# Depthwise convolution tiles moved from tap-by-tap VectorE operations to products on TensorE's column quarters

## The chip, the cores and the metric

One core of a Trainium2 chip runs the whole program. The metric is the device time of one execution in microseconds (us), lower is better. The engines named here are TensorE (PE, with its weight loads as PEld), VectorE (DVE), ScalarE (ACT), GpSimd (POOL) and SyncE (SP), whose queue issues most DMAs.

## The reference

Two blocks follow each other. The first has two layers over 528 tokens (16 of them meta tokens, padded further in the reference); each layer makes one projection, splits it, runs a causal depthwise convolution of width 31 over 512 channels and a sparse attention (top-k keys per query), and joins both through `w_out`. The second block has window attention, a gated linear attention and 16 experts. The change touches the convolution of the first block:

```
proj = jnp.einsum('bld,de->ble', h, w_in[l])
a, g, zc, q, k, v, za, qi, ki, wi = jnp.split(proj, IN_SPLITS, axis=-1)
u = a * jax.nn.sigmoid(g)
u = lax.conv_general_dilated(u, w_dw[:, None, :], window_strides=(1,),
        padding=[(CONV_WIDTH - 1, 0)], dimension_numbers=('NWC', 'WIO', 'NWC'),
        feature_group_count=D_CONV) + b_dw
u = jax.nn.silu(layer_norm(u, ln_g, ln_b))
return u * jax.nn.silu(z)
```

So each of the 512 channels is convolved by itself: 31 multiply-adds per output, no sum over channels.

## The kernel before

Channels lie on partitions, tokens along the free axis. The 512 convolution channels are four tiles of 128 (c = 0 to 3). The first layer carries 528 tokens through this part, the second 512. `p_ag(c)` computes one tile: the projections a and g (96 products at L181 with split weights: a weight tile `raw` is loaded at L151, ACT casts it to `wh` at L159, DVE takes the rest `wl` at L160), then ACT's `th` (L339) and DVE's `u` (L340), the gated input, with zeros ahead of it. Then `conv_tap(c, j)` is called 31 times and builds `cv[:, c]` in one of two ways:

- tiles in the set `pconv`: ACT multiplies (L323) and POOL adds (L325), tile after tile. `pconv` is (0, 1, 2) in layer 0 and (0, 1) in layer 1.
- the other tiles: one DVE operation per tap (L328 for the first, L330 for the other 30). These are tile 3 in layer 0, and tiles 3 and 2 in layer 1.

Everything else of the layer competes for the same engines. `topk` (L413, L414) is a long series on DVE. The attention runs in four pieces; in each, scores go through `burst` (L252, L258) into `pidx`, DVE reduces them (L585, `smb`), ACT takes the exponential (L590), PE transposes (L558) and multiplies by v (L565), and DVE ends the piece at L507 (`yas`). The tail of a layer reads `cv` (L650, L655), then the product with `w_out` follows. The weight tiles move in a fixed order on SP's queue, each load waiting until the buffer `raw` is free, which is when `wl` of an earlier tile is done.

The order on each engine is not that of the source: pieces of the program have levels (`plan`, `levels`, `go`), and a scheduler lays the instructions out by level before the run. In layer 0 the convolution tiles come in the order 2, 3, 1 after tile 0, with topk between them; in layer 1 in the order 1, 0, 3, 2. PE's two buffers named `pp` hold projection results until they are read.

Of the kernel before, what the change touches and what calls it, by code (L numbers as in the profile page):

```python
# [13 lines left out]
AF = mybir.ActivationFunctionType  # L14
ALU = mybir.AluOpType
AX = mybir.AxisListType
# [6 lines left out]
L = S + NM  # L23
KT = D // 128
W31 = 31
PAD = W31 - 1
ALPHA = 4.0 ** 0.25
TOPK = min(256, L // 4)
BIG = 1e30
# [39 lines left out]
class Net:  # L69
# [202 lines left out]
    def layer(self, l):  # L272
        nc, I = self.nc, self.I
        w_in, w_out = I["w_in"][l], I["w_out"][l]
        hT = self.hT
        q0 = 0 if l == 0 else NM
        T = L - q0
# [18 lines left out]
            nc.tensor.transpose(pcv[:, c, :], cw[:, c * 128:(c + 1) * 128], self.ident[:34, :34])  # L296
        cvec = self.sb([128, 4, 34], "cvec")
        nc.vector.tensor_copy(cvec, pcv)
        taps = self.sb([128, 4, 31], "taps")
        nc.vector.tensor_scalar(taps, cvec[:, :, 0:31], 0.5, None, op0=ALU.mult)  # L300

        pgb = self.sb([16, 128], "pgb", "rl", 3)
        nc.scalar.dma_start(pgb[0:8], I["post_ln_g"][l:l + 1].rearrange("o (t p) -> (o t) p", p=128))
# [11 lines left out]
        prod = []  # L315

        def conv_tap(c, j):
            src = u[:, c, j + q0:j + q0 + T]
            if c in pconv:
                if not prod:  # L320
                    prod.append(self.sb([128, 2, L], "prod", "zM"))
                pr = prod[0][:, j % 2, :T] if j else cv[:, c, :]
                nc.scalar.activation(pr, src, AF.Identity, scale=taps[:, c, j:j + 1], bias=0.0 if j else cvec[:, c, 31:32])  # L323
                if j:
                    nc.gpsimd.tensor_tensor(cv[:, c, :], cv[:, c, :], pr, op=ALU.add)  # L325
                return
            if j == 0:
                nc.vector.tensor_scalar(cv[:, c, :], src, taps[:, c, 0:1], cvec[:, c, 31:32], op0=ALU.mult, op1=ALU.add)  # L328
            else:
                nc.vector.scalar_tensor_tensor(cv[:, c, :], src, taps[:, c, j:j + 1], cv[:, c, :], op0=ALU.mult, op1=ALU.add)  # L330

        def p_ag(c):
            self.go("ag")
            ps = []
            for n in ("a", "g"):
                raw = self.load_w(w_in, WCOL[n] + 128 * c, 128)
                ps.append(self.proj(self.split_w(raw), 128, hT, KT, fsegs))
            th = self.sb([128, L], "th", "rl", 3)
            nc.scalar.activation(fseg(th), ps[1], AF.Tanh, scale=0.5)  # L339
            nc.vector.scalar_tensor_tensor(fseg(u[:, c, PAD:]), fseg(th), 1.0, ps[0], op0=ALU.add, op1=ALU.mult)  # L340
            self.go("conv")
            for j in range(W31):
                conv_tap(c, j)

# [74 lines left out]
        def topk_short(i):  # L419
            w = NM + 128 * (i + 1)  # L420
            out = w - TOPK
            acc = accs[i][:, :w]
            tk = self.sb([128, 3, w + 8], "tk", "up")
            n, e, c = (tk[:, k] for k in range(3))
            m8 = self.sb([128, 8], "m8", bufs=4)
            v = self.sb([128, 1], "tkv")
            pad = -out % 8
            nc.vector.memset(n[:, w:w + 8], 3e38 if pad else NEG_MARK)
            nc.vector.tensor_scalar(n[:, :w], acc, -1.0, None, op0=ALU.mult)
            for r in range((out + pad) // 8):  # L430
                nc.vector.max(m8, n[:, :w + pad])
                if r < (out + pad) // 8 - 1:
                    nc.vector.match_replace(n[:, :w + pad], m8, n[:, :w + pad], NEG_MARK)
            nc.vector.tensor_scalar(m8[:, 7:8], m8[:, 7:8], -1.0, None, op0=ALU.mult)
            n, e, c = (t[:, :w] for t in (n, e, c))
            nc.vector.tensor_scalar(n, acc, m8[:, 7:8], 0.0, op0=ALU.is_gt, op1=ALU.add, accum_out=v)
            nc.vector.tensor_scalar(v, v, -1.0, float(TOPK), op0=ALU.mult, op1=ALU.add)
            nc.vector.tensor_scalar(e, acc, m8[:, 7:8], None, op0=ALU.is_equal)
            nc.vector.tensor_tensor_scan(c, e, e, 0.0, op0=ALU.add, op1=ALU.bypass)
            nc.vector.scalar_tensor_tensor(e, c, v, e, op0=ALU.is_le, op1=ALU.mult)  # L440
            nc.vector.tensor_add(n, n, e)
            nc.vector.scalar_tensor_tensor(acc, n, BIG, self.c1[:, 3, L - w:], op0=ALU.mult, op1=ALU.add)
# [1232 lines left out]
    def first_block(self):  # L1675
        nc, I = self.nc, self.I
        self.ident = self.sb([128, 128], "base")
        nc.sync.dma_start(self.ident, I["c_base"])
        z = self.sb([128, 4, D], "z", "qk")
        zM = self.sb([NM, D], "zM")  # L1680
        nc.sync.dma_start(zM, I["meta_tokens"])
        for i in range(4):
            nc.sync.dma_start(z[:, i, :], I["x"][0, 128 * i:128 * (i + 1), :])
        self.c1 = self.sb([128, 4, L], "c1")
        nc.scalar.dma_start(self.c1, I["c_1"].rearrange("p (a b) -> p a b", a=4))
        self.new_hT()
        self.transposes_to(*self.hT, 0, zM, NM)
        for i in range(4):
            self.transposes_to(*self.hT, NM + 128 * i, z[:, i, :])
        for l in range(2):  # L1690
            self.cur = None
            self.layer(l)
# [26 lines left out]
```

## Time and profile before

| what | value |
|---|---|
| median of 3 runs | 1849.26 us (1848.18 to 1853.11) |
| the profiled execution, its own time | 1850.64 us |
| its span | 1848.8 us |
| mean granted clock of TensorE in it | 0.965 |

The profiled execution's time is its span and 1.8 us around it. Stages named in the text are stretches of the span in us: layer 0's attention ends near 327, layer 1's near 688, and the second block fills the rest.

### The profile page before, as it was taken

To read this page: it belongs to the slowest core of one execution; us is meant where nothing else is said; L and a number is where in the kernel's file an instruction comes from. 1 tells how busy PE (TensorE), PEld (TensorE's weight loads), DVE (VectorE), ACT (ScalarE), POOL (GpSimd) and SP (SyncE) were. 2 spreads that over 40 slices of the span, in tenths; PEclk is the share of its full clock that TensorE was granted. 3 is DMA by queue.
4 is the path that set the end of the run, shared out by engine and by line. 5 is a ranking of instruction groups with operands and counts; after the bars stand their busy time and mean duration, and the time that the engine had idled before them with its cause. 6 is when DMAs were issued, how large, how long until landed. Compare 5 with 4: busy or idle time off the path is not lost.

```text
span 1848.8 us, 27815 instructions
## 1 busy us (share of the span) xinstructions
PE 1686.7 (91%) x11323; PEld 1342.3 (73%) x11323; DVE 1010.8 (55%) x1947; ACT 765.4 (41%) x1310; POOL 238.0 (13%) x161
## 2 busy tenths in 40 slices
PE   6989989889998899799999999999899988888888
PEld 6989877889997789799888899999533332233246
DVE  3899994666998985775533445543401221012044
ACT  3874656447666554634355444322300000000026
POOL 1620863000068400000000000000000000000000
PEclk9999989999999899899989999999999999999999
DMA  6213111121222112222122248556799999999961
GB/s 194 69 47 93 46 46 46 30 70 59 69 61 79 46 47 81 89 69 91 36 63 75 76 143 288 158 211 230 280 421 421 421 420 421 421 420 421 419 273 46
DMA packets 147104, 323.35 MB, mean 175 GB/s; under 512 B 13034, under 2 KB 102826, under 8 KB 128672
## 3 DMA queue, kind: packets, MB, share of 16 engines
q1 hardware_dynamic: 142112, 310.54, 45.3%
q10 hardware_dynamic: 3856, 7.37, 1.1%
q0 software_dynamic: 1008, 3.67, 0.5%
q8 instruction: 89, 1.46, 0.3%
q14 instruction: 39, 0.32, 0.1%
HBM read 305.22 MB, written 16.25 MB: 174 GB/s over the span
## 4 chain that ended last, share of the span: by engine, by line
PE 58%; DMA 17%; DVE 15%; ACT 6%; issue 3%; POOL 1%; SPq 0%; ACTq 0%; DVEq 0%; POOLq 0%
PE pp L181 36%; PE pp L1571 7%; DMA rawe<-in_w_exp_down 7%; DMA rawe<-in_w_exp_gate 4%; DMA rawe<-in_w_exp_up 4%; DVE cv L330 3%; PE pp L1631 2%; DVE wl L160 2%; POOL cv L325 1%; ACT wh L159 1%; DVE smb L585 1%; PE po L565 1%; DVE acc L414 1%; DMA rawe<-in_w_ple_gate 1%; DVE m L413 1%
## 5 line engine op out<-in xcount | busy, mean ns | idle before, releaser
L325 POOL TENSOR_TENSOR cv<-cv,prod 128x528 f32<-128x528 f32 (+1 forms) x150 | 231.1, 1541 | 393.7 <-ACT prod L323 385.0
L1571 PE MATMUL pp<-rawe,xf 128*64 128x512 f32 x1024 | 247.8, 600 | 12.7 <-DMA rawe<-in_w_exp_gate 8.6
L181 PE MATMUL pp<-hTh,wh 128*128 128x264 f32 (+2 forms) x1056 | 227.4, 296 | 22.9 <-ACT th L339 8.0
L159 ACT CAST wh<-raw 128x1024 fp32r<-128x1024 f32 (+2 forms) x149 | 150.9, 1016 | 229.7 <-PE pp L181 204.0
L181 PE MATMUL pp<-hTl,wh 128*128 128x264 f32 (+2 forms) x1056 | 226.9, 295 | 0.1
L181 PE MATMUL pp<-hTh,wl 128*128 128x264 f32 (+2 forms) x1056 | 224.6, 293 | 0.0
L160 DVE TENSOR_TENSOR wl<-raw,wh 128x1024 fp32r<-128x1024 f32 (+2 forms) x149 | 187.5, 1259 | 65.9 <-ACT wh L159 59.2
L181 PEld LDWEIGHTS pp<-hTh,wh 128*128 128x128 f32 (+1 forms) x1056 | 170.9, 195 | 29.7 <-ACT th L339 9.3
L1571 PEld LDWEIGHTS pp<-rawe,xf 128*64 128x64 f32 x1024 | 76.8, 137 | 158.5 <-issue 131.0
L181 PEld LDWEIGHTS pp<-hTl,wh 128*128 128x128 f32 (+1 forms) x1056 | 170.7, 195 | 7.5 <-issue 6.7
L181 PEld LDWEIGHTS pp<-hTh,wl 128*128 128x128 f32 (+1 forms) x1056 | 169.8, 194 | 2.2 <-issue 1.6
L181 PE MATMUL pp<-xTh,wh 128*128 128x264 f32 (+1 forms) x752 | 156.3, 289 | 2.8 <-ACT op L1000 2.3
L181 PE MATMUL pp<-xTl,wh 128*128 128x264 f32 (+1 forms) x752 | 156.5, 288 | 0.5 <-DVE xTl L1095 0.5
L181 PE MATMUL pp<-xTh,wl 128*128 128x264 f32 (+1 forms) x752 | 155.2, 286 | 0.0
L1571 PE MATMUL pp<-rawe,hid 128*64 128x512 f32 x512 | 127.6, 616 | 18.6 <-DMA rawe<-in_w_exp_down 18.1
L1460 DVE SCALAR_TENSOR_TENSOR Y<-pp,per,Y 128x512 fp32r<-128x512 f32 x16 | 12.0, 749 | 232.7 <-ACT Y L1459 232.7
L1428 POOL DMA_INDIRECT xr<-xrows,slots x7 | 6.7, 958 | 993.2 <-DMA xrows<-zr 699.5
L323 ACT ACTIVATE prod<-u,taps 128x528 f32<-128x528 f32 (+1 forms) x150 | 107.6, 729 | 50.4 <-POOL cv L325 50.0
L181 PEld LDWEIGHTS pp<-xTh,wh 128*128 128x128 f32 (+1 forms) x752 | 116.8, 190 | 4.8 <-ACT op L1000 2.5
L181 PEld LDWEIGHTS pp<-xTl,wh 128*128 128x128 f32 (+1 forms) x752 | 116.2, 189 | 3.1 <-issue 2.2
L181 PEld LDWEIGHTS pp<-xTh,wl 128*128 128x128 f32 (+1 forms) x752 | 116.1, 189 | 0.8 <-issue 0.8
L1571 PEld LDWEIGHTS pp<-rawe,hid 128*64 128x64 f32 x512 | 40.6, 141 | 99.5 <-issue 61.0
(504 smaller groups left out, 2972.1 us busy)
## 6 DMA issues: line engine op xcount, KB each, us to landing
rawe<-in_w_exp_gate SPq DMA_DIRECT2D x53, 1024.0 KB, 16.3
rawe<-in_w_exp_up SPq DMA_DIRECT2D x52, 1024.0 KB, 15.0
rawe<-in_w_exp_down SPq DMA_DIRECT2D x51, 1024.0 KB, 19.6
raw<-in_w_in SPq DMA_DIRECT2D x45, 1024.0 KB, 5.3
rawe<-in_w_exp_down SPq DMA_DIRECT2D x26, 512.0 KB, 15.5
rawe<-in_w_exp_up SPq DMA_DIRECT2D x22, 512.0 KB, 16.2
rawe<-in_w_exp_gate SPq DMA_DIRECT2D x22, 512.0 KB, 17.4
raw<-in_w_in SPq DMA_DIRECT2D x20, 512.0 KB, 6.5
```

The costliest lines, as they stand in the source:

```text
L159: nc.scalar.copy(wh, raw_view)
L160: nc.vector.tensor_sub(wl, raw_view, wh.bitcast(F32))
L181: nc.tensor.matmul(ps[:m, s, x:min(x + k, n)], a[:, t, :m], b[:, c0 + x:min(c0 + x + k, c1)], start=(t == 0 and pi == 0 and x == 0), stop= ...
L323: nc.scalar.activation(pr, src, AF.Identity, scale=taps[:, c, j:j + 1], bias=0.0 if j else cvec[:, c, 31:32])
L325: nc.gpsimd.tensor_tensor(cv[:, c, :], cv[:, c, :], pr, op=ALU.add)
L330: nc.vector.scalar_tensor_tensor(cv[:, c, :], src, taps[:, c, j:j + 1], cv[:, c, :], op0=ALU.mult, op1=ALU.add)
L413: nc.vector.max(m8, acc)
L414: nc.vector.match_replace(acc, m8, acc, NEG_MARK)
L565: nc.tensor.matmul(po[:, h, :], pT[:, x * (i + 1) + j, :], v[:, j, h * 64:(h + 1) * 64], start=first[0], stop=False, skip_group_check=True)
L585: nc.vector.tensor_tensor_reduce(sm[:, x, :], pss[p][:, x, :], acc[:, NM:w], 1.0, mi[:, h:h + 1], ALU.add, ALU.max, mx[:, h:h + 1])
L1571: nc.tensor.matmul(ps[a, s, :], x[:, a], r, start=(t == 0 and k == 0), stop=(t == KT - 2 and k == 1), skip_group_check=True)
L1631: nc.tensor.matmul(ps[k][:, k, :], a[:, t, :], wp[t][:, w, k * 512:(k + 1) * 512], start=(t == 0 and pi == 0), stop=(t == KT - 1 and pi == 2))
```

## The change

`pconv` now says only which tiles go tap by tap on ACT and POOL. The other three go to `conv_products(c)`. It writes the convolution as products with diagonal operands. The 31 taps are padded to 32 with one zero (so the zeros ahead of `u` grow by one column), and read as 8 rounds of 4 taps. For each group g of 32 channels the 128 rows of the array hold four copies of these channels, each shifted by one more token (`us`, made by 16 DMAs from SP of 32 partitions each), and the operand for round e is 128 x 32: four diagonals stacked, with the taps 4e to 4e+3 (`cwt`, made by 16 small products and one DVE operation). A product of 32 output channels uses 32 columns of the array, a quarter; the four groups go to the four quarters. A tile takes two halves of the tokens x 8 rounds x 4 groups = 64 float32 products, in two `burst`s of 32, into one `pp` buffer, and ACT copies the sum with the bias to `cv`.

```diff
-PAD = W31 - 1
+PAD = W31
+CQ = 4
...
         def conv_tap(c, j):
-            src = u[:, c, j + q0:j + q0 + T]
-            if c in pconv:
...
-            if j == 0:
-                nc.vector.tensor_scalar(cv[:, c, :], src, taps[:, c, 0:1], cvec[:, c, 31:32], op0=ALU.mult, op1=ALU.add)
-            else:
-                nc.vector.scalar_tensor_tensor(cv[:, c, :], src, taps[:, c, j:j + 1], cv[:, c, :], op0=ALU.mult, op1=ALU.add)
...
+        def conv_products(c):
+            n = T // 2
+            nx = T + W31 + 1 - CQ
+            pt = self.ps([128, 4, 8], "pcv")
+            for g in range(4):
+                for k in range(CQ):
+                    nc.tensor.matmul(pt[32 * k:32 * k + 32, g, :], self.ident[:, 32 * g:32 * g + 32], taps[:, c, k::CQ], start=True, stop=True)
+            w = self.sb([128, 4, 8, 32], "cwt", "k2l")
+            nc.vector.tensor_tensor(w.rearrange("p g e c -> p (g e) c"), self.mask32[:, None, :].to_broadcast([128, 32, 32]),
+                                    pt.rearrange("p g e -> p (g e)")[:, :, None].to_broadcast([128, 32, 32]), op=ALU.mult)
+            us = [self.sb([128, 2, nx], "us", "sm", 2) for _ in range(2)]
+            for g in range(4):
+                for k in range(CQ):
+                    nc.sync.dma_start(us[g // 2][32 * k:32 * k + 32, g % 2, :], u[32 * g:32 * g + 32, c, k + q0:k + q0 + nx])
+            ps = self.ps([128, 2, 512], "pp", "pp", 2)
+            for k in range(2):
+                products = []
+                for e in range(8):
+                    for g in (3, 2, 1, 0):
+                        x0 = CQ * e + n * k
+                        products.append(((ps[32 * g:32 * g + 32, k, :n], w[:, g, e, :], us[g // 2][:, g % 2, x0:x0 + n]),
+                                         dict(start=e == 0, stop=e == 7, skip_group_check=True)))
+                self.burst(products)
+            nc.scalar.activation(cv[:, c, :].rearrange("p (k n) -> p k n", k=2), ps[:, :, :n], AF.Identity, scale=1.0, bias=cvec[:, c, 31:32])
...
             self.go("conv")
+            if c not in pconv:
+                conv_products(c)
+                return
```

The copies `us` take both buffers of the tag `sm`, which the attention's `smb` uses too. The rest of the diff moves two small tiles to other buffers and makes the 32-wide mask once.

The change moves instructions on the engines that meet here. On VectorE, at the end of layer 1's topk, the order of before has the attention's first reductions (L585) among the last steps of topk:

```order
L549 TENSOR_REDUCE mi<-smm_6270 128x8
L414 MATCH_REPLACE acc<-m_6079,acc 128x532
L413 MAX m_6042<-acc 128x8
L585 ISA smb,mx<-pidx,acc,mi 128x384
L585 ISA mx 128x1
L413 MAX m_6079<-acc 128x8
```

In the order of the change, topk ends first (L441 to L443), then come weight remainders, the two `u` of tiles 3 and 2 with `cwt` between them, and only then the attention's first reduction (now L612):

```order
L441 MATCH_REPLACE acc<-m_6227,acc 128x532
L442 TENSOR_SCALAR acc<-acc 128x272
L442 TENSOR_SCALAR acc<-acc 128x528
L443 TENSOR_TENSOR acc<-acc,c_72 128x272
L443 TENSOR_TENSOR acc<-acc,c_72 128x528
L161 TENSOR_TENSOR wl<-raw,wh 128x1024
L364 SCALAR_TENSOR_TENSOR u<-th,pp 128x528
L339 TENSOR_TENSOR cwt<-mask_146,pcv 128x1024
L161 TENSOR_TENSOR wl<-raw,wh 128x1024 x2
L364 SCALAR_TENSOR_TENSOR u<-th,pp 128x528
L612 ISA smb,mx<-pidx,acc,mi 128x384
```

So the attention of layer 1 moves behind both product tiles on VectorE. On PE, behind the projections of tile 3 and eight pairs of products of tile 2, the 64 products of tile 3 (`pp<-us,cwt`) now stand, with projections on both sides (the last rows before them and the first behind them):

```order
L182 MATMUL pp<-hTl,wh 128x264 x2
L182 MATMUL pp<-hTh,wl 128x264 x2
L253 MATMUL pp<-us,cwt 32x256
L259 MATMUL pp<-us,cwt 32x256 x31
L253 MATMUL pp<-us,cwt 32x256
L259 MATMUL pp<-us,cwt 32x256 x31
L182 MATMUL pp<-hTh,wh 128x264 x2
L182 MATMUL pp<-hTl,wh 128x264 x2
```

Those of tile 2 stand 65 instructions of the listing's L182 kind and one pair of scores later, and layer 0 has one such place, 16 products behind the projections of its tile 3. On ACT the copy of the sum (L354) of layer 1's tile 3 stands among the taps of the ACT tiles (L325), and the cast of a later weight tile (L160, the second half of tile 2's projections) behind five more taps:

```order
L325 ACTIVATE prod<-u,taps 128x512 x17
L354 ACTIVATE cv<-pp,cvec 128x512
L325 ACTIVATE prod<-u,taps 128x512 x5
L160 CAST wh<-raw 128x1024
L325 ACTIVATE prod<-u,taps 128x512 x2
L160 CAST wh<-raw 128x1024
L363 ACTIVATE th<-pp 128x528
L354 ACTIVATE cv<-pp,cvec 128x512
```

So an instruction that PE's projections wait for now stands behind one that waits for the convolution's products.

## Rows read from the trace of the kernel before

**Rows 1.** The page, section 1: busy us, share of the span, instructions.

```profile
PE 1686.7 (91%) x11323; PEld 1342.3 (73%) x11323; DVE 1010.8 (55%) x1947; ACT 765.4 (41%) x1310; POOL 238.0 (13%) x161
```

**Rows 2.** Windows: PE, PEld, DVE, ACT, POOL busy (x), PEclk, DMA share, GB/s.

```profile
200.00:225.00 25.00, 22.75 (x172) 21.74 (x172) 25.00 (x57) 17.96 (x34) 23.75 (x15) 0.92 0.14 43
...
250.00:275.00 25.00, 20.34 (x115) 18.16 (x116) 24.89 (x44) 10.44 (x22) 16.53 (x11) 0.80 0.13 43
...
600.00:625.00 25.00, 18.95 (x126) 16.63 (x124) 24.89 (x30) 14.47 (x34) 19.57 (x13) 0.90 0.14 43
```

**Rows 3.** Tile `cv`: line, engine, out<-in xcount: ns min/median/max, first and last start.

```profile
L325 POOL TENSOR_TENSOR cv<-cv,prod x150: 1268/1468/3352, 40.0 to 623.6; 128x528 f32<-128x528 f32 x90, 128x512 f32<-128x512 f32 x60
L330 DVE SCALAR_TENSOR_TENSOR cv<-u,taps,cv x90: 726/752/1883, 204.0 to 672.6; 128x512 f32<-128x512 f32 x60, 128x528 f32<-128x528 f32 x30
```

**Rows 4.** Windows of 25 us, L330 alone: one row, and the sum of eleven.

```profile
200.00:225.00 25.00, 7.87 (x7) 0.92 0.14 43
...
...
sum 275.00, DVE 89.64; mean DVE 8.15
```

**Rows 5.** Windows: two full stretches of projections, and the stretches around the tiles.

```profile
140.00:170.00 30.00, 30.00 (x254) 29.71 (x253) 29.38 (x81) 12.16 (x24) 0.00 (x0) 1.00 0.28 72
196.90:327.30 130.40, 115.94 (x827) 103.80 (x825) 103.30 (x213) 83.53 (x167) 81.26 (x52) 0.92 0.13 41
360.00:390.00 30.00, 30.00 (x251) 29.91 (x250) 17.17 (x40) 8.43 (x15) 0.00 (x0) 1.00 0.34 106
545.50:705.10 159.60, 142.02 (x1064) 128.20 (x1062) 140.38 (x303) 94.87 (x187) 68.07 (x45) 0.95 0.19 60
```

**Rows 6.** Timeline of PE at the second block's router products (start, us, instruction).

```profile
1261.23 1.06 PE L1317 MATMUL plog<-res,wr 128*32 128x512 f32 x6
1262.22 0.39 PE L181 MATMUL pp<-mh,wh 128*128 128x264 f32 x1
```

**Rows 7.** The same place: timeline of the weight loads, and the tile `plog`.

```profile
1261.23 0.15 PEld L1317 LDWEIGHTS plog<-res,wr 128*32 128x32 f32 x6
...
L1317 PEld LDWEIGHTS plog<-res,wr x16: 106/108/110, 1261.2 to 1289.0; 128*32 128x32 f32 x16
L1317 PE MATMUL plog<-res,wr x16: 592/604/617, 1261.2 to 1289.4; 128*32 128x512 f32 x16
```

**Rows 8.** Timeline of SP's queue: small copies between weight loads.

```profile
148.78 1.25 SPq L481 DMA_DIRECT2D vM<-vm  x2
153.02 0.37 SPq L151 DMA_DIRECT2D raw<-in_w_in  x1
```

**Rows 9.** DMA view: issues, KB each, median us from issue to landing.

```profile
vM<-vm SPq DMA_DIRECT2D x16, 4.0 KB, 2.2
h1d<-h SPq DMA_DIRECT2D x8, 256.0 KB, 2.3
```

**Rows 10.** Windows of 5 us around a stop of PE (the column behind POOL is PEclk).

```profile
110.00:115.00 5.00, 2.26 (x11) 2.27 (x11) 5.00 (x8) 3.16 (x5) 2.64 (x2) 0.65 0.01 2
115.00:120.00 5.00, 5.00 (x30) 5.00 (x30) 4.94 (x9) 4.32 (x9) 0.13 (x1) 0.66 0.16 33
```

**Rows 11.** Timeline of VectorE in layer 0: tile 3's `u`, and the end of topk.

```profile
200.72 0.69 DVE L340 SCALAR_TENSOR_TENSOR u<-th,pp 128x528 f32<-128x528 f32 x1
...
235.64 1.23 DVE L416 TENSOR_TENSOR acc<-acc,c 128x528 f32<-128x528 f32 x1
```

**Rows 12.** Timeline of VectorE in layer 1: `wl` behind topk, and the last two `u`.

```profile
575.77 1.22 DVE L160 TENSOR_TENSOR wl<-raw,wh 128x1024 fp32r<-128x1024 f32 x1
587.60 0.73 DVE L340 SCALAR_TENSOR_TENSOR u<-th,pp 128x528 f32<-128x528 f32 x1
615.85 0.69 DVE L340 SCALAR_TENSOR_TENSOR u<-th,pp 128x528 f32<-128x528 f32 x1
```

**Rows 13.** Source L507 in layer 0 and in layer 1: first and last end of an attention piece.

```profile
L507 DVE TENSOR_TENSOR yas<-po,rs x4: 670/678/692, 235.0 to 326.7; 128x512 f32<-128x512 f32 x4
L507 DVE TENSOR_TENSOR yas<-po,rs x4: 674/678/682, 594.1 to 686.8; 128x512 f32<-128x512 f32 x4
```

More of the change, by code (lines that the diff above doesn't have):

```diff
@@ L298, in layer @@
         nc.vector.tensor_copy(cvec, pcv)
-        taps = self.sb([128, 4, 31], "taps")
-        nc.vector.tensor_scalar(taps, cvec[:, :, 0:31], 0.5, None, op0=ALU.mult)
+        taps = self.sb([128, 4, W31 + 1], "taps")
+        nc.vector.memset(taps[:, :, 0:1], 0.0)
+        nc.vector.tensor_scalar(taps[:, :, 1:], cvec[:, :, 0:31], 0.5, None, op0=ALU.mult)
         pgb = self.sb([16, 128], "pgb", "rl", 3)
@@ L317, in conv_tap @@
         def conv_tap(c, j):
-            src = u[:, c, j + q0:j + q0 + T]
-            if c in pconv:
[L320 to L326, printed above, removed]
@@ L327, in conv_tap @@
-            if j == 0:
-                nc.vector.tensor_scalar(cv[:, c, :], src, taps[:, c, 0:1], cvec[:, c, 31:32], op0=ALU.mult, op1=ALU.add)
-            else:
-                nc.vector.scalar_tensor_tensor(cv[:, c, :], src, taps[:, c, j:j + 1], cv[:, c, :], op0=ALU.mult, op1=ALU.add)
+            src = u[:, c, j + 1 + q0:j + 1 + q0 + T]
+            if not prod:
+                prod.append(self.sb([128, 2, L], "prod", "zM"))
+            pr = prod[0][:, j % 2, :T] if j else cv[:, c, :]
+            nc.scalar.activation(pr, src, AF.Identity, scale=taps[:, c, j + 1:j + 2], bias=0.0 if j else cvec[:, c, 31:32])
@@ new lines, in conv_tap @@
+            if j:
+                nc.gpsimd.tensor_tensor(cv[:, c, :], cv[:, c, :], pr, op=ALU.add)
+        def conv_products(c):
[22 more added lines that the diff above has]
+            nc.scalar.activation(cv[:, c, :].rearrange("p (k n) -> p k n", k=2), ps[:, :, :n], AF.Identity, scale=1.0, bias=cvec[:, c, 31:32])
@@ L425, in topk_short @@
             m8 = self.sb([128, 8], "m8", bufs=4)
-            v = self.sb([128, 1], "tkv")
+            v = self.sb([128, 1], "tkv", "am")
             pad = -out % 8
@@ L1689, in first_block @@
             self.transposes_to(*self.hT, NM + 128 * i, z[:, i, :])
+        self.mask32 = self.sb([128, 32], "mask32", "xr")
+        nc.vector.tensor_reduce(self.mask32, self.ident.rearrange("p (s c) -> p c s", s=4), axis=AX.X, op=ALU.add)
         for l in range(2):
```

## The prediction

> **What bounds the kernel now.** I read the page's busy shares first: PE 91% of the span, DVE 55% [rows 1]. These are averages, so I next cut the stretches where the convolution runs into windows. There the picture turns: in 200 to 225, 250 to 275 and 600 to 625 VectorE is busy for 24.9 to 25.0 us of 25, while PE is busy for 19 to 23 us and its granted clock stands at 0.80 to 0.92 [rows 2]. PE waits for VectorE there, and the convolution is one of the reasons: 90 operations of line L330, 726 to 1883 ns each [rows 3], 89.6 us in all by windows [rows 4], about 30 in layer 0 (one tile) and 60 in layer 1 (two), plus the three first taps.
>
> How much could PE gain at most? Where PE is never idle at full clock, it retires 254 or 251 instructions in 30 us, 0.118 to 0.12 us each [rows 5]. Between the end of layer 0's `u` of tile 3 and the end of its attention, 196.9 to 327.3, it retires 827 in 130.4 us [rows 5]: 97.6 us of work at 0.118, so 32.8 us are idle or run at a low clock. From 545.5 to 705.1, where layer 1's product with `w_out` starts, it retires 1064 in 159.6 us [rows 5]: 125.6 us of work, 34.0 us slack. Together 66.8 us: that is what the change can win, before it adds anything.
>
> **The change, part by part.** *Removed:* 93 VectorE operations, 92 us with the first taps. VectorE was full there, so its other work moves up; but what this is worth is limited by the slack above, and only if PE doesn't get new waits.
>
> *Products on PE.* The trace has no float32 product of 264 columns on a quarter, but a near row: the router's products are 128 x 32 by 512 columns, float32, on four quarters. Six records (each product leaves two records, one per pass, and some are missing) begin at 1261.23 and end 1.06 us later, and the next product starts at 1262.22 [rows 6], so four products of 512 columns take 0.99 us side by side, although one record alone is 604 ns [rows 7]. With 264 or 256 columns I scale to 0.51 us a round. A tile has 2 halves x 8 rounds = 16 rounds: 8.2 us. The lower bound is the same (the rows have no faster one); one after another it would be four times that, 33 us, a rival below. The 16 small products for `cwt` are 8 columns each; at the 0.12 us of any PE instruction at most 2 us, I take 1. So 9.2 us for a tile, 27.6 for three.
>
> The Trainium skill, page "TensorE: Matmul & The Clock Gate", section "Part 3: Packing small matmuls — row/col tiling", says that a weight load overlaps products in flight only when the row group differs; here every product uses all 128 rows. By it each quarter's load would stand in the open. The row says otherwise: six loads of 106 to 110 ns lie within 0.15 us while the products run [rows 7], so I add nothing for loads. By the rule the sum would be about 10 us more; that case is a rival below.
>
> *The copies.* This is new on the path: between `u` and the first product there are now 16 DMAs from SP. Two small copies issue in 1.25 us on this queue, a weight load in 0.37 us [rows 8], so 16 take 5.9 to 10.0 us; a copy lands 2.2 us (4 KB) to 2.3 us (256 KB) after its issue [rows 9]. That bounds `u` to first product at 8.1 to 12.2 us; I take 10.5, nearer to the small copies, which they resemble. On SP they are queued behind the weight loads, which wait for `wl`, and the next weight load waits behind all 16. `cwt`, of the size of `wl` (1.22 us [rows 12]), lies beside the copies.
>
> What covers this? In the order, PE has 16 projection products behind tile 3's projections in both layers, then the burst: 2 us of cover. PE is in order, so it stands for 8 to 9 us. After a stop of this kind the granted clock fell to 0.65 and 0.66 for two windows of 5 us [rows 10], the lower of the two levels for a good part of them: 3.4 us lost. A tile thus costs 9 + 3.4 + 9.2 us, about 22.
>
> *Layer 0 (tile 3).* `u` is made at 200.7 now [rows 11]; I put it at 199, as the attention's reductions no longer stand ahead. Copies land at 209.5, the burst ends near 221. On ACT the copy L354 stands behind 19 taps that POOL paces at 1.27 to 1.47 us each [rows 3], 24 to 28 us, so to 223 to 227, and the cast of a weight tile behind it and four exponentials; PE has 32 products, 4 us, before it needs that cast: 1 to 7 more us of waiting, I take 5. Sum 27 against a slack of 32.8, so PE alone would end at 196.9 + 97.6 + 27 = 321.5 instead of 327.3. The attention starts later, but with VectorE free: topk ended at 236.9 [rows 11]; without the taps before it (7.87 us until 225 [rows 4], some 4 behind it) and the reductions it ends near 220. The last three pieces took 235.0 to 326.7, 91.7 us [rows 13], with about 20 us of the tile's taps among them; with a first piece of some 20 us the end lies between 220 + 20 + 72 = 312 and 332. I take 325: **-2 us**, bounds -6 (PE) to +10.
>
> *Layer 1 (tiles 3 and 2).* Here the order matters more. `u` of tile 3 now stands directly behind topk and one `wl`: 577 instead of 587.6 [rows 12], 10 us earlier. Copies land at 587.5, the products end near 598 with the low clock. Then the cast for tile 2's second half stands on ACT behind L354 and five taps: 0.8 + 6, 605. PE finishes tile 2's projections near 611, `u` follows at 613 or 614 (now 615.8 [rows 12], so all 10 us are gone). Copies land at 624, with 2 us of PE work (17 products) as cover; the products end near 634. VectorE idles through most of 578 to 634, as all attention stands behind the second `u`. Before that point PE has done 3 x 96 projections and some 30 others of the stretch, 318 x 0.118 = 37.5 us; 125.6 - 37.5 = 88 us remain to `w_out`. Without any further wait it starts at 722, 17 us later than at 705.1. The lower bound is lower: copies at 8.1 and no low clock give 4 to 5 us back for each tile, so +6. Some waits remain, as four attention pieces must run in these 88 us, which took 552 to 686.8 with taps in between (the last three 92.7 us [rows 13]); 6 us more is a choice between none and the 20 that would make the pieces as long as before less the taps. **+23 us**, bounds +6 to +38.
>
> *Sum.* -2 + 23 = +21 on the profiled execution's 1850.6: 1871.6. The profile lies 1.4 above the median of the runs, so 1870. The bounds give 1849 to 1897.
>
> **The rivals.** *The freed VectorE wins (faster).* If the copies land within about 3 us of `u`, with the 2 us of cover PE hardly stops, the clock stays up, and of the 66.8 us slack only 27.6 is spent: up to 39 us faster, 1810; half of it carried, 1830. It decides at a gap of 3 us from `u` to the first product. For it: VectorE full [rows 2]. Against: the issue times [rows 8]. Chance 0.18.
>
> *The stalls fall into idle time that stood anyway (no change).* If PE's stops replace the waits for VectorE one for one, layer 0 ends 6 earlier and layer 1 6 later, near 1849. For it: the slack of 34 us is spread over the same stretch. Chance 0.11.
>
> *The quarters don't run side by side.* Then a tile costs 33 us, 25 more for each of three: about 1945. The router's row speaks against it; but its products number 8, here 64 stand in a row and accumulate. Chance 0.05.
>
> *Weight loads in the open.* If a load waits for the products in flight, each of 32 passes pays 0.108 us [rows 7]: 3.5 us a tile, 10 in all, 1880. Chance 0.04. It is what the Trainium skill's sentence above amounts to.
>
> **How the numbers follow.** My forecast has 0.62, with a range of its own of 1852 to 1896. For 8 in 10 the range must reach down to the half-carried gain: 1832 to 1896; the serial quarters and the better half of the gain stay out. A measurement of this kernel tells about 0.3%, 5.5 us, from no change. Faster: the first rival and a little of the second, 0.19. Same: most of the second and the edge of the forecast, 0.11. Slower: the rest, 0.70.
>
> **What would show it.** In the changed profile: L344 in SP's queue 16 times in 6 to 10 us and PE idle for 8 to 9 us before L253/L259 `pp<-us,cwt`, released by the DMA; that burst 8 to 12 us; a lower granted clock behind it; VectorE with idle stretches near 580 to 630; the first L612 of layer 1 near 630; layer 0's last L534 near 325. It is wrong if the DMA gap is short, if the burst takes another time than 8 us at full clock, or if the attention behind it runs much faster, or slower, than I let it.

## The result, and the profile after

The changed kernel takes 1897.34 us (median of 4 runs, 1894.89 to 1901.11) against 1850.52 for the kernel before: ratio 1.0254, 95% interval 1.0230 to 1.0278. It is 47 us slower where 20 were forecast, just above the range. One execution of e4 below took 2732 us at a mean granted clock of 0.567; the ratios leave it out.

The page's first section answers to [rows 1]. VectorE gave up 83.5 us, PE took 17 more, and the span grew by 48.1:

```profile
PE 1703.8 (90%) x11803; PEld 1354.8 (71%) x11803; DVE 927.3 (49%) x1860; ACT 770.1 (41%) x1312; POOL 220.1 (12%) x161
```

Where the time went shows best if the span is cut where the program passes the same instruction in both traces. The cuts are the start of the last product with `w_out` of each layer (`ych` or `ycl`), the first small router product (`plog<-pick`), and the 301st product of the experts (`pp<-rawe,xf`):

| stage | before, us | after, us | difference |
|---|---|---|---|
| start to the end of layer 0 | 392.9 | 392.8 | -0.1 |
| layer 1 | 359.4 | 400.5 | +41.2 |
| second block to the router | 539.1 | 533.5 | -5.6 |
| router to the 301st expert product | 125.5 | 136.4 | +10.9 |
| the rest | 432.1 | 433.7 | +1.6 |

Layer 1 and the router stage hold the loss. (The third stage lies between 533.4 and 541.4 us over all fourteen traces of this case, 539.1 before and 537.1 in the fastest kernel, so its -5.6 us is not put down to the convolution.)

The timeline of PE in the changed kernel, first products of the three tiles (start, length, instruction, and in brackets the idle time before it and what ended it):

```profile
210.39 0.62 PE L253 MATMUL pp<-us,cwt 128*32 128x264 f32 x1 [15.46 <-ACT prod L325]
...
590.64 0.61 PE L253 MATMUL pp<-us,cwt 128*32 128x256 f32 x1 [16.97 <-DMA us<-u]
...
591.27 5.67 PE L259 MATMUL pp<-us,cwt 128*32 128x256 f32 x59
...
596.97 3.42 PE L259 MATMUL pp<-us,cwt 128*32 128x256 f32 x59
...
627.69 0.60 PE L253 MATMUL pp<-us,cwt 128*32 128x256 f32 x1 [14.40 <-DMA us<-u]
```

Before each burst PE stands for 14 to 17 us; nothing of the kind stood in the trace before. (For layer 0 the releaser named is ScalarE's `prod`, which the products don't read; it is the last semaphore event before, and the copies landed then.) The first half of a tile takes 5 to 6 us, the second 3.7 to 3.8. The windows say why (PE, PEld, DVE, ACT, POOL busy, then PEclk, DMA share, GB/s):

```profile
580.00:585.00 5.00, 0.00 (x0) 0.00 (x0) 0.00 (x0) 2.52 (x5) 4.69 (x5) 0.50 0.47 111
...
590.00:595.00 5.00, 4.36 (x41) 3.85 (x45) 0.00 (x0) 2.89 (x4) 4.69 (x5) 0.50 0.01 4
595.00:600.00 5.00, 5.00 (x90) 4.73 (x84) 0.00 (x0) 2.17 (x3) 4.69 (x5) 0.92 0.00 0
```

The granted clock fell to 0.50, the lower level (1.2 GHz), in the stop, and the first half of the products ran at it. VectorE was idle too, 0.00 of 5 us, as its own timeline shows (the first line is of the kernel before, the rest answers to [rows 12]):

```profile
L585 DVE CUSTOM_DVE_ANT_0 smb<-pidx,acc,mi x4: 587/592/603, 551.8 to 557.5; 128x384 f32<-128x384 f32 x4
...
578.23 0.69 DVE L364 SCALAR_TENSOR_TENSOR u<-th,pp 128x528 f32<-128x528 f32 x1
600.47 1.22 DVE L339 TENSOR_TENSOR cwt<-mask,pcv 128x1024 f32<-128x1024 f32 x1 [21.55 <-PE pp L259]
...
615.32 0.70 DVE L364 SCALAR_TENSOR_TENSOR u<-th,pp 128x528 f32<-128x528 f32 x1
637.71 0.62 DVE L612 CUSTOM_DVE_ANT_0 smb<-pidx,acc,mi 128x384 f32<-128x384 f32 x1 [21.69 <-PE pp L259]
```

The attention's first reduction waits for the last product L259 of the second tile: 637.71 instead of 551.8. (The wait of 21.55 us above it is for another buffer: `cwt` of tile 2 has to take the one that tile 3's products still read. The kernels below leave that one as it is.) SP's queue in the same stretch, and L507 of [rows 13] as it is now (L534):

```profile
578.99 10.01 SPq L344 DMA_DIRECT2D us<-u  x16
...
616.09 10.01 SPq L344 DMA_DIRECT2D us<-u  x16
...
L534 DVE TENSOR_TENSOR yas<-po,rs x4: 669/688/693, 250.6 to 326.6; 128x512 f32<-128x512 f32 x4
...
L534 DVE TENSOR_TENSOR yas<-po,rs x4: 674/691/691, 666.2 to 735.0; 128x512 f32<-128x512 f32 x4
```

16 copies take 10.0 us to issue. Layer 0's attention ends where it did, layer 1's 48 us later. In layer 0 topk ends sooner, at 211.5 instead of 236.9 [rows 11], and the first reduction waits for the same buffers there:

```profile
208.27 3.26 DVE L443 TENSOR_TENSOR acc<-acc,c 128x272 f32<-128x272 f32 x2
219.36 0.62 DVE L612 CUSTOM_DVE_ANT_0 smb<-pidx,acc,mi 128x384 f32<-128x384 f32 x1 [7.83 <-PE pp L259]
```

### The profile page after: what moved, and what is told of

Its sections match the earlier page's. It is cut to its first block, busy times and chain, and to the rows that moved or that the text cites. A ratio compares the mean times of both kernels' runs of the same rounds, so it can differ in the third digit from the quotient of the medians.

```text
span 1896.9 us, 28780 instructions
## 1 busy us (share of the span) xinstructions
PE 1703.8 (90%) x11803; PEld 1354.8 (71%) x11803; DVE 927.3 (49%) x1860; ACT 770.1 (41%) x1312; POOL 220.1 (12%) x161
## 4 chain that ended last, share of the span: by engine, by line
PE 58%; DMA 24%; DVE 8%; ACT 5%; issue 2%; POOL 1%; SPq 1%; ACTq 0%; DVEq 0%; POOLq 0%
PE pp L182 39%; DMA rawe<-in_w_exp_up 9%; DMA rawe<-in_w_exp_gate 7%; DMA rawe<-in_w_exp_down 6%; PE pp L1658 2%; PE pp L1598 2%; PE po L592 2%; DVE wl L161 2%; POOL cv L327 1%; PE tp L585 1%; PE pp L259 1%; SPq L344 1%; PE pidx L253 1%; ACT wh L160 1%; DVE acc L441 1%
## 5 line engine op out<-in xcount | busy, mean ns | idle before, releaser
L1598 PE MATMUL pp<-rawe,xf 128*64 128x512 f32 x1024 | 252.4, 607 | 10.9 <-DMA rawe<-in_w_exp_gate 6.6
L327 POOL TENSOR_TENSOR cv<-cv,prod 128x528 f32<-128x528 f32 (+1 forms) x150 | 213.2, 1422 | 398.6 <-ACT prod L325 390.0
L160 ACT CAST wh<-raw 128x1024 fp32r<-128x1024 f32 (+2 forms) x149 | 151.1, 1017 | 224.6 <-PE pp L182 193.4
L182 PE MATMUL pp<-hTh,wh 128*128 128x264 f32 (+2 forms) x1056 | 223.8, 291 | 17.6 <-ACT th L363 7.3
L182 PE MATMUL pp<-hTl,wh 128*128 128x264 f32 (+2 forms) x1056 | 219.7, 288 | 0.0
L182 PE MATMUL pp<-hTh,wl 128*128 128x264 f32 (+2 forms) x1056 | 218.7, 287 | 0.0
L1598 PEld LDWEIGHTS pp<-rawe,xf 128*64 128x64 f32 x1024 | 79.0, 139 | 159.6 <-issue 131.7
L182 PEld LDWEIGHTS pp<-hTh,wh 128*128 128x128 f32 (+1 forms) x1056 | 165.9, 190 | 24.8 <-issue 8.3
L182 PEld LDWEIGHTS pp<-hTl,wh 128*128 128x128 f32 (+1 forms) x1056 | 165.3, 189 | 6.2 <-issue 5.8
L182 PEld LDWEIGHTS pp<-hTh,wl 128*128 128x128 f32 (+1 forms) x1056 | 164.8, 189 | 1.6 <-issue 0.9
L182 PE MATMUL pp<-xTh,wh 128*128 128x264 f32 (+1 forms) x752 | 153.8, 285 | 2.8 <-ACT op L1027 2.3
L182 PE MATMUL pp<-xTl,wh 128*128 128x264 f32 (+1 forms) x752 | 154.8, 285 | 0.7 <-DVE xTl L1122 0.7
L182 PE MATMUL pp<-xTh,wl 128*128 128x264 f32 (+1 forms) x752 | 154.4, 283 | 0.0
L325 ACT ACTIVATE prod<-u,taps 128x528 f32<-128x528 f32 (+1 forms) x150 | 107.6, 729 | 55.1 <-POOL cv L327 53.8
L182 PEld LDWEIGHTS pp<-xTh,wh 128*128 128x128 f32 (+1 forms) x752 | 115.2, 189 | 4.6 <-ACT op L1027 2.5
L182 PEld LDWEIGHTS pp<-xTl,wh 128*128 128x128 f32 (+1 forms) x752 | 115.0, 188 | 3.6 <-issue 2.5
L182 PEld LDWEIGHTS pp<-xTh,wl 128*128 128x128 f32 (+1 forms) x752 | 115.0, 188 | 0.8 <-issue 0.8
## 6 DMA issues: line engine op xcount, KB each, us to landing
rawe<-in_w_exp_down SPq DMA_DIRECT2D x26, 512.0 KB, 15.5
```

The source lines that it names most:

```text
L160: nc.scalar.copy(wh, raw_view)
L182: nc.tensor.matmul(ps[:m, s, x:min(x + k, n)], a[:, t, :m], b[:, c0 + x:min(c0 + x + k, c1)], start=(t == 0 and pi == 0 and x == 0), stop= ...
L1598: nc.tensor.matmul(ps[a, s, :], x[:, a], r, start=(t == 0 and k == 0), stop=(t == KT - 2 and k == 1), skip_group_check=True)
```

## The experiments

The theories: **A**, the 16 serial copies stop PE; **B**, the copies take both buffers of the attention's tile, so no attention can start and nothing is there to fill the stop; **P**, PE has no room in layer 1, so that each us of products, idle time and low clock there counts; **R**, the router stage lost its time to another order of ScalarE. The table has medians, the ratio to the kernel before, and the two layers' times, which come from one profiled execution each:

| run | us | ratio, 95% | end of layer 0 | layer 1 |
|---|---|---|---|---|
| before | 1850 | 1 | 392.9 | 359.4 |
| changed | 1897.3 | 1.0254 (1.0230-1.0278) | 392.8 | 400.5 |
| e1_router_order | 1892.7 | 1.0224 (1.0201-1.0248) | 393.0 | 397.7 |
| e2_free_buffers | 1859.9 | 1.0051 (1.0034-1.0068) | 385.8 | 375.9 |
| e3_four_copies | 1871.6 | 1.0110 (1.0089-1.0131) | 388.0 | 392.5 |
| e4_layer0_only | 1854.9 | 1.0019 (1.0005-1.0032) | 394.4 | 362.3 |
| e5_half_rounds | 1859.5 | 1.0054 (1.0037-1.0071) | 387.7 | 366.8 |
| e6_products_later | 1849.5 | 0.9999 (0.9985-1.0012) | 383.1 | 370.5 |
| e7_layer0_free | 1845.8 | 0.9972 (0.9961-0.9984) | 388.7 | 360.5 |
| e8_later_two_queues | 1841.1 | 0.9951 (0.9934-0.9968) | 382.7 | 360.9 |
| e9_router_full | 1890.9 | 1.0225 (1.0204-1.0246) | 395.4 | 394.3 |
| e10_later_attention_buffers | 1878.4 | 1.0155 (1.0136-1.0174) | 400.1 | 380.1 |
| e11_layer1_tile3 | 1842.4 | 0.9956 (0.9941-0.9970) | 381.0 | 365.0 |
| e12_layer1_tile2 | 1858.8 | 1.0048 (1.0032-1.0064) | 381.5 | 375.1 |

**The router's order (e1, e9).** In ScalarE's order of the changed kernel the second copy of the embedding product (`pe`) stands ahead of the second scaling of the router's rows (`zr`). Its timeline, and ahead of it the order in the kernel before:

```profile
1303.87 2.08 ACT L1358 ACTIVATE zr<-z,r 128x1024 f32<-128x1024 f32 x1 [5.68 <-DMA xrows<-zr]
1305.99 0.33 ACTq L1359 DMA_DIRECT2D xrows<-zr  x1
1307.90 1.01 ACT L787 COPY pe<-pp 128x1024 f32<-128x1024 f32 x1 [1.94 <-PE pp L785]
...
1333.72 0.33 ACTq L815 DMA_DIRECT2D pled<-pe  x1
1344.18 1.01 ACT L814 COPY pe<-pp 128x1024 f32<-128x1024 f32 x1 [10.49 <-PE pp L812]
1345.09 2.09 ACT L1385 ACTIVATE zr<-z,r 128x1024 f32<-128x1024 f32 x1
...
1361.52 0.33 ACTq L1386 DMA_DIRECT2D xrows<-zr  x1
```

ScalarE waits 10.5 us for PE's product with `zr` behind it; the last DMA of the rows goes out at 1361.52, and PE waits for what is gathered from them:

```profile
1369.79 0.45 PE L1462 MATMUL tp<-base,xr 128*128 128x128 f32 x1 [5.01 <-DMA xr<-xrows,slots]
```

e1 fixes the order of the copies behind `zr` (e9 behind its DMA):

```diff
-                nc.scalar.copy(pe.rearrange("p (a b) -> p a b", a=2), ps)
+                if i:
+                    with self.tc.issue_after(self.zr[i].ins):
+                        nc.scalar.copy(pe.rearrange("p (a b) -> p a b", a=2), ps)
+                else:
+                    nc.scalar.copy(pe.rearrange("p (a b) -> p a b", a=2), ps)
...
```

> Only the order of ScalarE in the second block's router stage is changed back to that of the kernel before: each copy of the embedding product stands behind the scaling of the router's rows (zr), as it did. Between the traces of before and of the change the distance grew from +35.5 us at the router's top-k to +46.6 us at the first expert products. Theory R (the order of these copies alone did that; the convolution has no part in it): the time falls by 9 to 11 us, from 1897 to about 1887, and the distance stays near +36 through the router. Rival (a lower clock or the weight transfers did it): the time stays within 3 us of 1897.

> As the first experiment, and now the copies of the embedding product stand behind the DMA of the router's rows too (xrows), which the first left behind such a copy (issued at 1342.99 us, 2.8 us after zr was done). Theory R (the order of ScalarE in the router stage holds up the gather of the rows, for which PE waited 5.0 us in the changed kernel): the distance to the kernel before no longer grows between the router's top-k and the first expert products (it grew 11 us in the changed kernel and 5 in the first experiment), and the time is 1886 to 1889, 8 to 11 us below 1897. Rival (it grows whatever stands there): 1893 or more.

Measured: 1892.7 and 1890.9, 4.7 and 6.4 us less, not 8 to 11. The router stage fell from 136.4 to 130.8 and 130.1 us, against 125.5 before. So ScalarE's order accounts for about 6 of the 10.9 us. For the other 4 or 5 the traces show a second change of order, on PE. Before, the experts' first products run while the gathered rows `xr` are still on their way; in e9, PE transposes those rows first, and waits for them:

```profile
1325.51 1.07 PE L1571 MATMUL pp<-rawe,xf 128*64 128x512 f32 x3
...
L1435 PE MATMUL tp<-base,xr x56: 270/272/330, 1346.3 to 1684.0; 128*128 128x128 f32 x56
...
1362.59 0.30 PE L1467 MATMUL tp<-base,xr 128*128 128x128 f32 x1 [2.52 <-DMA xr<-xrows,slots]
1362.82 1.08 PE L1603 MATMUL pp<-rawe,xf 128*64 128x512 f32 x4
```

The first two lines are of the kernel before, the others of e9. Counted from the router's product, the first expert product starts at 34.2 us before, at 43.4 in the changed kernel and at 38.9 in e9, though the last rows go out no later in e9 (25.8 us) than before (26.2). The transposes stand ahead in the changed kernel, e1, e9 and e5, whose stage takes 130.1 to 136.4 us, and behind 96 product records in the other ten, with 125.5 to 129.2. No run changed PE's order alone.

**Other buffers (e2).** 

```diff
-            us = [self.sb([128, 2, nx], "us", "sm", 2) for _ in range(2)]
+            us = [self.sb([128, 2, nx], "us", t) for t in ("qi", "szc")]
...
-        szc = self.sb([128, 4, T], "szc")
...
+            szc = self.sb([128, 4, T], "szc")
```

> The shifted copies lie in two buffers that are idle in this stretch (those of qi and szc, the tile szc being taken only where it is first written) and no longer in both buffers of the attention's tile smb. The 16 DMAs, the products and ScalarE's copy of the sum are unchanged, and the scheduler's order follows: the attention stands among the products again, and the router's copies stand as in the kernel before. Theory B (the buffers did it: as long as the copies hold them no attention can start, so nothing is there to fill PE's stop): PE's two stops in layer 1 of 17 and 14 us mostly vanish and the attention starts near 552 again; 30 to 45 us less together with the router's 11, so 1852 to 1867, and if VectorE's relief counts too, below 1850. Theory A (the 16 serial DMAs did it: 10 us of issuing plus landing between u and the first product stop PE wherever it stands): PE still stops 10 us or more per tile, and the time falls by little more than the router's 11 us, to about 1880 to 1886.

Measured 1859.9, within B's 1852 to 1867 and far from A's 1880. Layer 1 gave back 24.6 of its 41.2 us, and layer 0 now gains 7. The router stage is at 127.1. The copies still take 10 us from SP and nothing of PE's work is less. But layer 1 still loses 16.6 us, although PE is idle there for no more than 14.0 us between 530 and 725 (17.6 before). The clock shows the difference:

```profile
580.00:585.00 5.00, 5.00 (x27) 5.00 (x26) 2.51 (x5) 3.99 (x10) 3.84 (x4) 0.50 0.47 109
585.00:590.00 5.00, 5.00 (x23) 3.50 (x25) 1.27 (x3) 2.81 (x4) 4.76 (x4) 0.50 0.24 58
590.00:595.00 5.00, 5.00 (x72) 2.75 (x74) 3.73 (x19) 3.44 (x10) 4.69 (x5) 0.75 0.02 3
```

PE is called busy for 5.00 of 5 us, but at 0.50 and with 23 to 27 instructions instead of some 42: only the attention's short pieces stand in the wait for the copies.

**Fewer copies (e3).**

```diff
-                for k in range(CQ):
-                    nc.sync.dma_start(us[g // 2][32 * k:32 * k + 32, g % 2, :], u[32 * g:32 * g + 32, c, k + q0:k + q0 + nx])
+                nc.sync.dma_start(us[g // 2][:, g % 2, :], u[:, c, q0:q0 + nx])
```

> Four DMAs of 128 partitions instead of 16 of 32 for each tile: every copy then has the same shift, so the convolution computed is another one (the three tiles hold wrong sums); products, buffers and order of the changed kernel stay, except that the router's copies stand as in the kernel before. Theory A: the time between u and the first product falls by about 7.5 us per tile (12 issues of 0.63 us less), PE's stops in layer 1 go from 17 and 14 us to about 9.5 and 7, and with the router's 11 us the time falls to about 1870; layer 0 gives nothing more. Theory B: the same 15 us at most, for the attention still waits for both tiles, so far above 1850 even then. If the stops are set by something else (cwt, the casts), the time stays at 1886.

Measured 1871.6, near A's 1870, with 4 issues in 2.5 us and these stops, against 9.5 and 7 expected:

```profile
578.93 0.60 PE L253 MATMUL pp<-us,cwt 128*32 128x256 f32 x1 [10.12 <-DMA us<-u]
...
609.75 0.60 PE L253 MATMUL pp<-us,cwt 128*32 128x256 f32 x1 [8.27 <-DMA us<-u]
```

So the issue of the copies does count while nothing fills the stop: A and B are both true, and B weighs more (37 us less in e2, 26 here, the router's part in both). (The profiled execution took 1886.7 us, four of the other five 1869 to 1872. Where these 15 us lie isn't known, so of this trace only the stops are read. In its router stage `pe` stands ahead of the rows' DMA, so its order there is not quite that of before.)

**Layer 0 alone (e4, e7).** Both give layer 1's two tiles VectorE's taps back; e7 also has the free buffers.

> Layer 0 keeps its product tile, layer 1 has its two tiles tap by tap on VectorE as before. In the trace of the change layer 0's product with w_out started at 333.06 us against 333.12 before. Both theories: 1850 within 4 us, since layer 0's slack took the copies, and so all of the loss lies in layer 1 and in the router stage. If the layer 0 tile has a cost or a gain that shows only later, the time would differ from 1850 by more than 5 us.

> The free buffers, and products only for layer 0's tile; layer 1's two tiles tap by tap on VectorE as in the kernel before. In the run with free buffers in both layers layer 0's product with w_out started about 7 us earlier than before and layer 1 lost 16.6. Theory P (where VectorE's taps had left PE idle more than the products cost, a tile gains): 1843 to 1846, faster than before by 5 to 7 us. Rival (layer 0's 7 us are lost again in layer 1, where VectorE is the limit): 1850.

Measured 1854.9 and 1845.8. In the changed form layer 0's tile is worth nothing, rather a loss of 0.2% (1854.9 lies just outside the 1850 within 4 us that was expected); with free buffers it gains 0.28%. The first agrees with the table of stages: without layer 1's tiles layer 1 takes 362.3 us again and the router stage 125.5. The second bears P out for layer 0.

**Half of the products (e5).** On the kernel of e2:

```diff
-                for e in range(8):
+                for e in range(4):
...
-                                         dict(start=e == 0, stop=e == 7, skip_group_check=True)))
+                                         dict(start=e == 0, stop=e == 3, skip_group_check=True)))
```

> The kernel with the copies in free buffers, and only rounds 0 to 3 of the 8: half of the products, the other taps are left out of the sum (so the three tiles hold another convolution); copies, buffers and the order around the products are the same. In the run with all rounds layer 1 still ended 16.6 us later than before, although PE was idle for 14.0 us there against 17.6 before. Theory P (PE has no room in layer 1: the products' own time, 8 us per tile, and the low clock they meet are the cost): each tile falls by 3.6 to 4.5 us, so the product with w_out of layer 1 starts 10 to 13 us earlier and the time falls from 1860 to 1847 to 1851. Rival (the wait for the copies still sets the end, not the products): layer 1 ends where it did, and the time falls by less than 4 us.

Measured 1859.5, no less than e2, which by the time alone speaks for the rival. The two traces speak for P in layer 1, which fell from 375.9 to 366.8 us, 4.6 per tile against P's 3.6 to 4.5; its product with `w_out` started 7.6 us earlier, not 10 to 13. The gain was lost elsewhere: layer 0 ended 1.9 later, and the router stage took 132.5 instead of 127.1, where ScalarE's order (`pe` ahead of the rows' DMA) and PE's had moved again.

**The products later (e6, e8).** e6 writes the products behind projections; e8 also lets ScalarE's queue issue half of the copies:

```diff
-             ('idx', 'q', 'k', 'sc', 'ag1', 'v', 'ag0', 'ag3', 'topk', 'ag2', 'att', 'za', 'zc'),
+             ('idx', 'q', 'k', 'sc', 'ag1', 'v', 'ag0', 'ag3', 'topk', 'ag2', 'cp3', 'cp2', 'att', 'za', 'zc'),
...
-                    nc.sync.dma_start(us[g // 2][32 * k:32 * k + 32, g % 2, :], u[32 * g:32 * g + 32, c, k + q0:k + q0 + nx])
+                    (nc.sync, nc.scalar)[k % 2].dma_start(us[g // 2][32 * k:32 * k + 32, g % 2, :], u[32 * g:32 * g + 32, c, k + q0:k + q0 + nx])
```

> On top of the free buffers the products of a tile are written later in the program: in layer 0 behind the projections of tile 1, in layer 1 those of both tiles behind the projections of tile 2, so that projections (96 products, 11 us at full clock) stand between u and the products, where with free buffers alone the attention's short pieces stood at half clock. Theory P with the low clock: the stretches at 0.50 ahead of the products (205 to 220, 575 to 592, 630 to 641) go, 6 to 8 us each two stretches of layer 1 and 7 us of layer 0 partly; the time falls from 1860 to about 1848, level with before. If the low clock costs nothing there, since the products meet a full PE anyway, it stays at 1857 to 1860.

> The kernel with the products later, and the 16 copies issued in halves by SP and by ScalarE's queue. If the time from u to the first product still matters there, it falls from about 12 to 7 us and the time falls by 3 to 8 us against the kernel with one queue; if the projections cover the copies, the two are within 3 us of each other, or it is slower, since ScalarE's queue also carries the casts that PE waits for.

Measured 1849.5 and 1841.1: level with the kernel before, as P with the low clock had it, and 0.49% faster. In e8 the place that stood at half clock in e2 is at full clock:

```profile
580.00:585.00 5.00, 5.00 (x44) 4.99 (x44) 0.79 (x5) 3.79 (x11) 3.77 (x3) 1.00 0.73 223
585.00:590.00 5.00, 4.52 (x76) 3.19 (x79) 1.90 (x3) 3.92 (x8) 4.05 (x3) 1.00 0.01 4
```

and its first tile of layer 1 takes 3.5 us for the first half and 3.8 for the second with its end, with hardly a wait. The second tile still meets a stop and the low clock (the last three lines, the window with PEclk 0.74):

```profile
586.20 0.40 PE L253 MATMUL pp<-us,cwt 128*32 128x256 f32 x1 [0.48 <-ACT th L363]
...
586.63 3.40 PE L259 MATMUL pp<-us,cwt 128*32 128x256 f32 x57
589.68 0.38 PE L253 MATMUL pp<-us,cwt 128*32 128x256 f32 x1
...
589.90 3.62 PE L259 MATMUL pp<-us,cwt 128*32 128x256 f32 x61
...
602.86 0.27 ACT L633 COPY pT<-tp 128x128 f32<-128x128 f32 x1 [1.12 <-DMA us<-u]
...
603.17 2.08 PE L634 MATMUL po<-vM,pT 128*128 128x512 f32 x2 [5.70 <-ACT pT L633]
...
605.00:610.00 5.00, 5.00 (x70) 2.41 (x72) 1.52 (x5) 1.42 (x8) 0.00 (x0) 0.74 0.00 0
```

There the attention's copy `pT` stands on ScalarE behind the issues of the tile's own copies, the drawback that was named as possible for two queues. The 8.4 us that e8 gains on e6 lie just above the 3 to 8 expected, but neither kernel's first tile in layer 1 waits for its copies (0.72 and 0.48 us, both for `th`), so the shorter issue is not shown to be what gained them.

**The buffers again (e10).** e8 with the copies back in the attention's two buffers.

> The kernel with the products later and two queues (1841.1 us), but with the copies back in both buffers of the attention's tile smb. Theory B (the buffers hold up the attention, whatever stands around the products): layer 1 loses again what the free buffers gave, 20 us or more, and the time is 1860 to 1875, with VectorE idle in layer 1 until the second tile's products are done. Rival (the projections ahead of the products fill PE, so the buffers don't matter): 1841 to 1846.

Measured 1878.4, 37 us more than e8: the way B said, and 3 us above its 1860 to 1875. VectorE in layer 1:

```profile
598.09 0.69 DVE L364 SCALAR_TENSOR_TENSOR u<-th,pp 128x528 f32<-128x528 f32 x1
609.00 1.22 DVE L339 TENSOR_TENSOR cwt<-mask,pcv 128x1024 f32<-128x1024 f32 x1 [10.21 <-PE pp L259]
626.36 0.62 DVE L611 CUSTOM_DVE_ANT_0 smb<-pidx,acc,mi 128x384 f32<-128x384 f32 x1 [16.14 <-PE pp L259]
```

Again the first reduction waits for the last product, here 16.1 us. Layer 0 ends 17 us later than in e8, layer 1 takes 19 longer.

**One tile of layer 1 (e11, e12).** e8 with one tile of layer 1 on VectorE.

> The kernel with the products later and two queues, but in layer 1 only tile 3 as products and tile 2 tap by tap on VectorE. Theory P (layer 1 has room on PE for about as much as VectorE's 30 us of taps for a tile had cost it): one tile each is the better balance, 1835 to 1840. Rival (tile 2's taps are the late ones on VectorE, last at 672 us before, so leaving them there keeps the end): 1841 to 1846.

> As the run before, with tile 2 as products and tile 3 tap by tap on VectorE. Theory P: 1835 to 1840, and rather better than with tile 3, for VectorE is done with its taps earlier. Rival: the products of the last tile stand late, their copies are waited for at half clock as with both tiles, 1841 or more.

Measured 1842.4 and 1858.8, as the rivals had it: no balance tried is better than e8, the best kernel here. e11's interval overlaps e8's. In e12 PE waits for the attention in the middle of the taps:

```profile
596.55 1.63 PE L591 MATMUL tp<-base,smb 128*128 128x128 f32 x4 [6.27 <-ACT smb L623]
...
615.67 1.97 PE L598 MATMUL po<-v,pT 128*128 128x64 f32 x8 [10.06 <-ACT pT L594]
```

ScalarE is named there; its `pT` stands behind the issues of the tile's copies again (ScalarE's eight, 607.1 to 615.0). Whether VectorE's taps of tile 3 held the attention up ahead of that was not tried.

## Why the prediction was wrong

The direction was right, and so was one of its causes: a stop of PE between `u` and the products, at a granted clock that falls. Layer 0's number was right, in part by luck. Layer 1 was mis-sized and its larger cause not named, and one stage was missing. Against the forecast of +21 the profiled execution moved by +48.1: 18 us more in layer 1, 11 in the router stage, 2 in layer 0, and -4 in the other two stages of the table.

*Right.* The quarters run side by side: a half tile of 32 products takes 3.7 to 3.8 us at full clock, start to start, and a whole tile 7.3 in e8, against the 8.2 taken from the router's products. The Trainium skill, page "TensorE: Matmul & The Clock Gate", section "Part 3: Packing small matmuls — row/col tiling", says in one sentence that a weight load overlaps products in flight only with another row group; by that these loads would have shown. They don't: eight rounds of four products of 256 columns in 3.69 us are 0.46 us a round, less than half of the router's 0.99 for 512 columns. The loads take 110 ns each here and 108 there, so if they stood in the open, the narrow round would be dearer than half. (Each product has two records; what each stands for no row shows.)

*Right by two errors:* layer 0's -2 us was -0.1. Topk ended at 211.5, 8 us sooner than taken, but the attention then waited 7.8 us for the copies' buffers and began at 219.4, close to the 220 of the forecast. PE's stop was 15.5 us and not 8 to 9.

*The copies* were at the upper bound: 10.0 us of issuing and 2.0 to landing, 12.4 from the start of `u` to the first product against the 10.5 taken.

*"2 us of cover"* failed. In layer 1 the 16 projection products of tile 2 ran before `u` of tile 3 was ready, not after: they end at 573.67, `th` of tile 3 follows at 574.42 behind a cast, VectorE's `wl` (2.28 us) stands ahead of `u`, and `u` starts at 578.23. So PE stood for 15.5, 17.0 and 14.4 us instead of 8 to 9. A tile with the low clock took 8.9 to 9.9 us instead of 12.6, which gives part of it back, and the second burst ended at 637.6 instead of 634.

*"88 us remain to `w_out`"*, and 6 of waiting, failed most: it was 108.6, as the stretch from the end of the burst to the end of layer 1 shows, less the one that followed 705.1 before (PE busy, records, PEclk behind POOL):

```profile
637.60:793.40 155.80, 148.80 (x1179) 138.38 (x1176) 81.65 (x226) 72.69 (x152) 0.00 (x0) 0.97 0.17 49
...
705.10:752.30 47.20, 47.20 (x388) 47.20 (x388) 28.20 (x58) 14.64 (x20) 0.00 (x0) 0.96 0.27 71
```

Without 3 records of the burst itself, 788 remained and not 746: the 318 taken as done counted 42 too many. Idle time and the low clock took some 10 us of the 108.6 (7.0 idle and 3% of 155.8, less 4% of 47.2), where the forecast had 6. By this estimate the other 98.8 us are 0.125 for each record and not 0.118, which had been read where projections alone run. The attention's scores are dearer: four records of 384 columns in one place (604.29 to 605.13) took 0.21 each. With 3.6 us from the burst these make the 18 us by which layer 1 was missed. (705.1 is not where the product with `w_out` starts, as the prediction has it, but where it goes on after a wait of 2.85 us; its first records lie at 697.93, and at 739.53 in the changed kernel, 41.6 later. Nor is 196.9 the end of layer 0's `u` of tile 3, which starts at 200.72 [rows 11].)

Behind it stands the slack of 34 us. Of it PE was idle for 17.6 us only and some 8 lay at the low clock (0.95 over 159.6 us); the rest was the price of 0.118. With free buffers (e2) PE was idle for less and layer 1 still lost 16.6 us. How much could be won back depended on what stands around the products: in e8 layer 1 carries both tiles' products, some 15 us, and takes 1.5 us longer than before.

*Named, but not as a cause:* that the attention moves behind both tiles was in the order and in the sum. That only the copies' buffers force it was not in the prediction. Of layer 1's 41.2 us, 24.6 hang on that (e2), and e10 loses 19 there when the buffers are taken again.

*Missing:* the router stage, 10.9 us. The orders of ScalarE and PE had changed there as well, 700 us behind the last of the new products, and could be read before the run; the sum has no term for it.

The first rival (the freed VectorE wins) was right in this: with the wait filled, as in e8, the products are faster than VectorE's taps, but by 9 to 10 us and not by 20 to 40. Its own condition, copies within 3 us of `u`, held in no run.

## What to carry to other kernels

Before a wait is costed, look at which buffers the new tiles take: a tile that shares the buffers of another stage orders that whole stage behind itself, which cost 24.6 us of one layer here. In layer 1 the new chain of work on a full engine paid only where dense work of that engine stood between the chain's start and its end (e8, e11); filling it with short pieces (e2) kept PE busy by the record, at half the clock. And where a scheduler lays out the program, compare its order everywhere, not only at the edit.

## What the runs showed of the hardware

On SP's queue 16 copies of 32 partitions (67.5 KB each) took 10.0 us to issue, 0.63 each, and 4 copies of 128 partitions 2.5 us, 0.62 each: the issue time went by the number of DMAs. With two queues (e8), SP issued its 8 in 5.0 to 5.6 us, while ScalarE's 8 took 8.2 to 8.7 us among its other work. A round of float32 products of 256 columns on four quarters took 0.46 us at full clock (3.69 us for eight), 0.44 where the other half followed (3.48, e8). At the low clock (0.50, e2) PE was recorded busy for all of 5 us with 23 to 27 instructions, so that busy time alone did not show what was lost.
